# A decoder layer on one core: the second norm's sum formed where the residual's whole rows lie

## The chip, the core and the metric

One NeuronCore of a Trainium2 chip runs the whole program. TensorE (PE) multiplies matrices into PSUM, VectorE (DVE) and ScalarE (ACT) do elementwise work, GpSimd (POOL) does some elementwise work on SBUF and issues transfers, and the SP queue issues transfers only. The metric is the device time of one execution in microseconds (us); the lower, the better.

## The reference

One layer of a hybrid decoder over 2048 new prompt rows and 64 sample rows (8 sequences of 8), width 1024:

```
h = rmsnorm(x, pre_mix_w)
m = mixer(h)                       # retention heads and gated-delta heads, then w_out
x = x + rmsnorm(m, post_mix_w)     # the first residual sum, x1
h = rmsnorm(x, pre_mlp_w)          # the second norm, h2
f = square(relu(h @ w_up)) @ w_down
y = x + rmsnorm(f, post_mlp_w)
```

All of it is in float32 in effect: each operand of a large product is split into a high part and a low part, and three products are summed. The change touches only the two lines in the middle: x1 and h2.

## The kernel before

**Blocks.** The prompt is cut into four blocks of 512 rows (`Block`, b = 0 to 3), each of four tiles of 128 rows; block 1 also has the 64 sample rows as a fifth tile. `main` runs, for each block, the input projection merged with the MLP of the block before it (`merge(blk.proj(), prev.mlp())`), then `out_proj`, then the last group of the MLP's down projection of the block before (`mlp_down(NG - 1)`). After block 3 its own MLP follows.

**Order.** `Weave` is a planner: generators yield either a latency in ns or a key, and resume when the planner's clock, which matmuls advance, has reached it or the key has been signalled. This writes out TensorE's order by hand, and that order is kept. The instructions of the other engines are ordered by the framework's own scheduler, by priority in the order in which they were written; every engine runs its list in order, and a transfer stands in the list of the engine that issues it.

**Tiles.** `page` gives tiles with a tag. Tags that matter: `xin` (five buffers of half rows) takes first loads of weights, the next block's input, stored mixer rows and residuals; `wpc` (eight buffers) holds split weights; `ahi` and `alo` hold the high and low parts of h2, which the MLP reads, and in block 0 also those of the mixer's output; `fhi` and `flo` hold the MLP's features; `XX`, `mt`, `kv`, `ym` and `Ss` hold the tiles 0 to 4 of m. A new tile of a tag waits until all users of the one before it in that buffer are done.

**Weights.** `load_unit` loads a unit of weights the first time through `xin`, splits it (ACT the high part, POOL the low part) into `wpc`, and stores it to DRAM; later uses load the split form straight into `wpc`. The last group of `w_down` is first used behind the output projection of block 1.

**The output projection.** `out_proj` runs over four units u of 256 columns and the tiles in each. `evac` squares a result on ACT into `sq` and writes m, times the weights of the first norm, on DVE. After its last unit a tile's `norm2` is spawned. It loads the residual's row halves into two `xin` buffers (line 1305, POOL's queue), makes the reciprocal root of the mean square (POOL's power, `rsqrt`), forms x1 in place in m (line 1314), squares it on ACT into PSUM tiles of the tag `mx`, stores x1 to `x1d` for the end of the MLP (line 1316, POOL's queue), scales it in place to h2 (line 1323), transposes it on TensorE (line 1333) and writes high parts on ACT and low parts on DVE (line 1337). Its small numbers lie in `r1`, which has two buffers. `lat` gives the planner's latencies: n0 to n3 between these steps and h2 before the transposes.

**After it.** `finish_half` adds the stored x1 to the MLP's result: its loads of `x1d` also go into `xin` (line 1448).

Of the kernel before, what the change touches and what calls it, by code (L numbers as in the profile page):

```python
# [10 lines left out]
AF = mybir.ActivationFunctionType  # L11
ALU = mybir.AluOpType
AX = mybir.AxisListType

P = 128
D_MODEL = 1024
T = 512
NC = T // P
# [7 lines left out]
KT = D_MODEL // P  # L26
UNIT = 256
NU = 264
# [177 lines left out]
def hybrid_kernel(ctx: ExitStack, tc: tile.TileContext, I, O, NB: int, SB: int):  # L206
    nc = tc.nc
    PS = bass.MemoryType.PSUM
    NTM = T + NS
    WB = 8  # L210
    XB = 5
    LAG = 5
    HP = 100
    W = Weave()
# [13 lines left out]
    def nm(s):  # L228
        uid[0] += 1
        return f"{s}_{uid[0]}"  # L230

    def page(shape, tag, dt=F32, bufs=1):
        return wk.tile(shape, dt, tag=tag, name=nm(tag), bufs=bufs)

    def small(shape, tag, dt=F32, bufs=2):
        return sm.tile(shape, dt, tag=tag, name=nm(tag), bufs=bufs)

    def mm():
        return mmp.tile([P, 512], F32, tag="mm", name=nm("mm"))

    def mx():
        return mxp.tile([P, 512], F32, tag="mx", name=nm("mx"))
# [4 lines left out]
    def cut(t, n, w=1024):  # L247
        return [t[:, i * w:(i + 1) * w] for i in range(n)]
# [3 lines left out]
    def act(out, in_, f, **kw):  # L252
        return A.activation(out, in_, f, **kw)  # L253

    def stt(out, in0, scalar, in1, op0, op1):
        return V.scalar_tensor_tensor(out=out, in0=in0, scalar=scalar, in1=in1, op0=op0, op1=op1)  # L256

    def tt(out, a, b, op, eng=None):
        return (eng or V).tensor_tensor(out=out, in0=a, in1=b, op=op)  # L259
# [87 lines left out]
    def save(left):  # L347
        while len(unsaved) > left:
            nc.sync.dma_start(*unsaved.pop(0))

    def load_unit(name, idx, n, ncol):


        src = I[name]
        for i in idx:
            src = src[i]
        per = 2 if ncol <= NU else 1
        w = per * ncol
        first = (name, idx) not in stored
        if first:  # L360
            stored[name, idx] = [wst.tile([P, 2 * w], F32, tag=nm("ws"), name=nm("ws")) for q in range(n // per)]
        his, los = [], []
        for q in range(n // per):
            fit = lambda t: t.rearrange("p (a c) -> p a c", a=per)
            both = page([P, 4 * NU], "wpc", F32R, bufs=WB)
            hi, lo = fit(both[:, :w]), fit(both[:, w:2 * w])
            flat = both[:, :2 * w].bitcast(F32)
            if first:
                r = fit(page([P, 2 * NU], "xin", bufs=XB)[:, :w])
                nc.sync.dma_start(r, src[:, per * q:per * (q + 1), :])  # L370
                save(LAG)
                act(hi, r, AF.Copy)
                tt(lo, r, hi.bitcast(F32), ALU.subtract, eng=G)
                if NB > 1:
                    unsaved.append((stored[name, idx][q], flat))
            else:
                save(0)
                nc.sync.dma_start(flat, stored[name, idx][q])
            his.append(hi)
            los.append(lo)  # L380
        return (lambda k: his[k // per][:, k % per, :]), (lambda k: los[k // per][:, k % per, :])
# [43 lines left out]
    class Block:  # L425
# [828 lines left out]
        def out_proj(self, then=None):  # L1254
            tiles, nt = self.tiles, self.nt
            wB = []
            order = self.order
            for e in order[:6]:
                yield self.key(f"m{e}")
            for n, src in enumerate(("post_mix_w", "pre_mlp_w")):  # L1260
                w = page([P, D_MODEL], "kq", bufs=2) if self.b else page([P, D_MODEL], atag[n])
                nc.gpsimd.dma_start(w, I[src].to_broadcast([P, D_MODEL]))
                wB.append(w)
            m = []
            sq = small([P, 5, 4], "sq", bufs=1)

            def evac(ps, t, rows, u):
                act(mx()[:rows, :UNIT], ps[:rows, :UNIT], AF.Square, accum_out=sq[:rows, t, u:u + 1])
                cols = slice(u * UNIT, (u + 1) * UNIT)
                tt(m[t][:rows, cols], ps[:rows, :UNIT], wB[0][:rows, cols], ALU.mult)  # L1270

            for u in range(4):
                wu = load_unit("w_out", (u,), KT, UNIT)
                if u == 1 and then:
                    W.spawn(then(), W.t)
                held = []
                if u == 0:
                    for t, (c0, rows) in enumerate(tiles[:MMB]):
                        ps = mm()
                        yield from gemm_tm(ps[:rows, :UNIT], self.mix, wu, c0, rows, order[:6], last=False)  # L1280
                        held.append(ps)
                    for e in order[6:]:
                        yield self.key(f"m{e}")
                    m += [page([P, D_MODEL], htag[t]) for t in range(nt)]
                for t, (c0, rows) in enumerate(tiles):
                    if t < len(held):
                        ps = held[t]
                        yield from gemm_tm(ps[:rows, :UNIT], self.mix, wu, c0, rows, order[6:], first=False)
                    elif t == NC:
                        ps = yield from gemm_samp(UNIT, self.mix, wu)  # L1290
                    else:
                        ps = mm()
                        yield from gemm_tm(ps[:rows, :UNIT], self.mix, wu, c0, rows, order)
                    evac(ps, t, rows, u)
                    if u == 3:
                        W.spawn(self.norm2(t, m[t], sq, wB), W.t + self.lat["n0"])

        def norm2(self, t, m, sq, wB):
            c0, rows = self.tiles[t]
            mr = m[:rows]  # L1300
            r = small([P, 4], "r1")[:rows]
            rx = lambda i: r[:, i:i + 1]
            xs2 = [page([P, 2 * NU], "xin", bufs=XB)[:rows, :T] for hf in range(2)]
            for hf in range(2):
                nc.gpsimd.dma_start(xs2[hf], self.x_rows(t)[:, hf * T:(hf + 1) * T])
            with tc.high_priority(offset=HP):
                V.tensor_reduce(out=rx(0), in_=sq[:rows, t, :], axis=AX.X, op=ALU.add)
                tsc(rx(0), rx(0), 1.0 / D_MODEL, EPS, ALU.mult, ALU.add)
                rsqrt(rx(0), rx(0), 1)
            yield self.lat["n1"]  # L1310
            for hf in range(2):
                x = xs2[hf]
                mh = mr[:, hf * T:(hf + 1) * T]
                stt(mh, mh, rx(0), x, ALU.mult, ALU.add)
                act(mx()[:rows, :T], mh, AF.Square, accum_out=rx(2 + hf))
            nc.gpsimd.dma_start(self.x1d[c0:c0 + rows, :], mr)
            yield self.lat["n2"]
            with tc.high_priority(offset=HP):
                tt(rx(1), rx(2), rx(3), ALU.add)
                tsc(rx(1), rx(1), 1.0 / D_MODEL, EPS, ALU.mult, ALU.add)  # L1320
                rsqrt(rx(1), rx(1), 1)
            yield self.lat["n3"]
            stt(mr, mr, rx(1), wB[1][:rows], ALU.mult, ALU.mult)
            if t == self.nt - 1:
                W.signal(self.key("w"))
            yield self.lat["h2"]
            if t == 0:
                self.h2 = (page([P, KT, NTM], "ahi", F32R), page([P, KT, NTM], "alo", F32R))
            hhi, hlo = self.h2
            for kk in range(2):  # L1330
                pt = mx()
                for k in range(4):
                    transpose(pt[:, k * rows:(k + 1) * rows], mr[:, (4 * kk + k) * P:(4 * kk + k + 1) * P], rows)
                pv = pt[:, :4 * rows].rearrange("p (k i) -> p k i", k=4)
                hv = hhi[:, 4 * kk:4 * kk + 4, c0:c0 + rows]
                act(hv, pv, AF.Copy)
                tt(hlo[:, 4 * kk:4 * kk + 4, c0:c0 + rows], pv, hv.bitcast(F32), ALU.subtract)
            W.signal(self.key(f"h{t}"), 1.6 * US)
            if t == self.nt - 1:
                W.signal(self.key("n"))  # L1340
# [74 lines left out]

        def mlp(self):
            for g in range(NG):
                yield (self.key("h0"),) if g == 0 else ()
                yield from self.mlp_up(g)
                if g < NG - 1:  # L1420
                    yield ()
                    yield from self.mlp_down(g)
# [141 lines left out]
```

## Time and profile before

| | |
|---|---|
| Median of 3 runs | 2990.23 us (2987.69 to 2990.53) |
| Profiled execution | 2994.72 us, span 2992.9 us |
| TensorE busy | 2869.1 us, 96% of the span |
| DVE, ACT, POOL busy | 49%, 32%, 28% |
| Mean granted clock of TensorE | 0.98 of full speed |
| DMA traffic | 197 GB/s over the span |

A busy TensorE is not TensorE at its peak, since matmuls overlap. The clock has two levels, 1.2 and 2.4 GHz; a granted clock of 0.50 is the lower. In the rows below, `a<-b` reads "a is written from b", `L1305` is line 1305 of the kernel, and `X <- Y` in a list of waits means that X stood still until Y was done. L253, L256, L259, L264, L271 and L275 are the helpers for ACT's, DVE's and TensorE's instructions.

### The profile page before, as it was taken

What the parts mean: (1) busy time and instruction counts of PE and PEld (TensorE: products, weight loads), DVE (VectorE), ACT (ScalarE), POOL (GpSimd) and SP (SyncE); (2) the same over time, 40 slices, a digit from 0 to 9 for tenths busy, and PEclk for the clock granted to TensorE, in tenths of its full rate; (3) what the DMA queues carried; (4) which work ended last, traced back from release to release, by engine and by line L of the source; (5) the groups of instructions that cost most, each with busy time, mean ns of one, the idle gap of its engine ahead of it and who ended that gap; (6) DMA issues with size and microseconds to landing.
All of it is one profiled execution on the core that took longest, in us unless ns stands there. A gap on an engine that the chain in (4) does not pass through costs nothing.

```text
span 2992.9 us, 43660 instructions
## 1 busy us (share of the span) xinstructions
PE 2869.1 (96%) x16392; PEld 2488.7 (83%) x16392; DVE 1457.3 (49%) x3074; ACT 963.9 (32%) x2573; POOL 825.9 (28%) x968
## 2 busy tenths in 40 slices
PE   7999898999999889899999999999999999999998
PEld 6879787787977769788988989988888888888887
DVE  6754466547474572745354444365353534331113
ACT  4555433324343332422323232232222222321111
POOL 6444323536154360602021121131120212210000
PEclk9999898999999999999999999999999999999999
DMA  8454474656646564854445454675555555665554
GB/s 322 173 194 148 168 262 150 237 199 213 217 154 232 177 237 155 312 204 155 170 154 188 149 180 153 225 259 181 176 191 184 183 182 175 239 236 194 185 193 167
DMA packets 190610, 588.94 MB, mean 197 GB/s; under 512 B 26784, under 2 KB 33312, under 8 KB 190400
## 3 DMA queue, kind: packets, MB, share of 16 engines
q1 hardware_dynamic: 157520, 498.36, 47.9%
q0 software_dynamic: 31728, 85.71, 8.6%
q8 instruction: 129, 2.11, 0.3%
q10 hardware_dynamic: 1152, 2.10, 0.2%
q14 instruction: 81, 0.66, 0.1%
HBM read 443.09 MB, written 137.79 MB: 194 GB/s over the span
## 4 chain that ended last, share of the span: by engine, by line
PE 79%; DVE 9%; DMA 4%; issue 3%; POOL 2%; ACT 2%; SPq 0%; DVEq 0%; POOLq 0%; ACTq 0%
PE mm L271 68%; PE mx L271 9%; PE mx L275 2%; DVE XX L259 1%; DVE ym L259 1%; POOL wpc L259 1%; DMA x1d<-mt 1%; DMA xin<-in_w_down 1%; DVE a L259 0%; DMA xin<-in_x_prompt 0%; DMA xin<-in_xpT 0%; DMA XX<-ym 0%; DVE vz L256 0%; ACT junk L253 0%; DVE vzs L256 0%
## 5 line engine op out<-in xcount | busy, mean ns | idle before, releaser
L271 PE MATMUL mm<-ahi,wpc 128*128 128x512 f32 (+2 forms) x3040 | 876.6, 363 | 0.8 <-ACT ahi L253 0.8
L271 PE MATMUL mm<-wpc,fhi 128*128 128x512 f32 x2048 | 654.5, 400 | 13.1 <-DVE a L259 7.4
L271 PEld LDWEIGHTS mm<-ahi,wpc 128*128 128x128 f32 x3040 | 545.2, 190 | 79.5 <-issue 4.8
L271 PE MATMUL mm<-alo,wpc 128*128 128x512 f32 (+2 forms) x1520 | 539.4, 355 | 2.3 <-DVE alo L259 2.3
L271 PEld LDWEIGHTS mm<-wpc,fhi 128*128 128x128 f32 x2048 | 378.9, 189 | 105.9 <-DVE a L259 9.4
L271 PE MATMUL mm<-bhi,wpc 128*128 128x512 f32 (+2 forms) x1536 | 426.7, 353 | 0.0
L271 PE MATMUL mm<-wpc,flo 128*128 128x512 f32 x1024 | 406.2, 397 | 2.4 <-DVE flo L259 2.4
L259 POOL TENSOR_TENSOR wpc<-xin,wpc 128x512 fp32r<-128x512 f32 (+1 forms) x208 | 276.0, 1344 | 218.3 <-ACT wpc L253 197.5
L271 PEld LDWEIGHTS mm<-alo,wpc 128*128 128x128 f32 x1520 | 289.8, 191 | 35.4 <-DVE alo L259 2.7
L253 ACT ACTIVATE raw<-mm 128x512 f32<-128x512 f32 (+2 forms) x226 | 115.5, 511 | 609.4 <-PE mm L271 598.9
L271 PEld LDWEIGHTS mm<-bhi,wpc 128*128 128x128 f32 x1536 | 274.9, 191 | 33.7 <-issue 2.5
L271 PE MATMUL mm<-wpc,bhi 128*128 128x256 f32 (+1 forms) x1664 | 296.5, 284 | 1.2 <-ACT bhi L253 1.2
L259 DVE TENSOR_TENSOR a<-a,mm 128x512 f32<-128x512 f32 x224 | 152.3, 684 | 243.5 <-PE mm L271 243.0
L271 PE MATMUL mm<-blo,wpc 128*128 128x512 f32 (+2 forms) x768 | 266.2, 347 | 0.0
L259 DVE TENSOR_TENSOR flo<-raw,fhi 128x512 fp32r<-128x512 f32 (+1 forms) x166 | 105.6, 636 | 305.6 <-ACT raw L253 305.2
L271 PEld LDWEIGHTS mm<-wpc,bhi 128*128 128x128 f32 x1664 | 250.4, 188 | 1.9 <-ACT bhi L253 1.4
L271 PEld LDWEIGHTS mm<-wpc,flo 128*128 128x128 f32 x1024 | 193.6, 189 | 48.1 <-DVE flo L259 3.3
L271 PE MATMUL mm<-wpc,blo 128*128 128x256 f32 (+1 forms) x768 | 215.2, 280 | 0.4 <-DVE blo L259 0.4
L253 ACT ACTIVATE wpc<-xin 128x512 fp32r<-128x512 f32 (+1 forms) x208 | 130.0, 630 | 185.8 <-PE mm L271 121.3
L271 PEld LDWEIGHTS mm<-blo,wpc 128*128 128x128 f32 x768 | 146.8, 191 | 14.6
L271 PEld LDWEIGHTS mm<-wpc,blo 128*128 128x128 f32 x768 | 144.6, 188 | 0.9 <-DVE blo L259 0.9
L259 POOL TENSOR_TENSOR a<-a,vz 128x512 f32<-128x512 f32 x28 | 36.5, 1318 | 339.3 <-ACT mx L253 339.0
(504 smaller groups left out, 3987.2 us busy)
## 6 DMA issues: line engine op xcount, KB each, us to landing
wpc<-ws SPq DMA_DIRECT2D x612, 512.0 KB, 4.9
ws<-wpc SPq DMA_DIRECT2D x204, 512.0 KB, 5.8
xin<-in_w_up SPq DMA_DIRECT2D x64, 256.0 KB, 5.4
xin<-in_w_down SPq DMA_DIRECT2D x64, 256.0 KB, 5.0
xin<-in_x_prompt POOLq DMA_DIRECT2D x56, 256.0 KB, 5.1
xin<-in_w_ret SPq DMA_DIRECT2D x28, 256.0 KB, 5.0
wpc<-ws SPq DMA_DIRECT2D x12, 528.0 KB, 5.0
mixd<-raw POOLq DMA_DIRECT2D x24, 256.0 KB, 4.6
```

Source lines behind the costliest of these rows:

```text
L253: return A.activation(out, in_, f, **kw)
L259: return (eng or V).tensor_tensor(out=out, in0=a, in1=b, op=op)
L271: return tc.keep_in_program_order(nc.tensor.matmul(out, lhsT, rhs, start=start, stop=stop))
L275: return tc.keep_in_program_order(nc.tensor.transpose(out, in_, ident[:rows, :rows]))
```

## The change

At the start of unit 1 of the output projection one transfer for each tile loads the residual's whole rows, on POOL's queue: in blocks 1 to 3 into the place of `alo` (the sample rows into that of `ahi`), in block 0 into those of `fhi` and `flo`. `norm2` gets its part as `xr`. It forms x1 there in place of in m, squares it and stores it from there, and the scaling writes h2 from `xr` into m. A count `left` signals a new key `x` when the scaling of the last tile has been written out; the transposes of every tile, and the start of the MLP, wait for that key. In blocks 1 to 3 the tiles for h2's parts reuse the residual's places, in block 0 the tiles for the first features do.

```diff
--- before.py
+++ after.py
@@ -1263,6 +1263,7 @@
                 wB.append(w)
             m = []
             sq = small([P, 5, 4], "sq", bufs=1)
+            self.left = nt
 
             def evac(ps, t, rows, u):
                 act(mx()[:rows, :UNIT], ps[:rows, :UNIT], AF.Square, accum_out=sq[:rows, t, u:u + 1])
@@ -1270,6 +1271,16 @@
                 tt(m[t][:rows, cols], ps[:rows, :UNIT], wB[0][:rows, cols], ALU.mult)
 
             for u in range(4):
+                if u == 1:
+
+                    if self.b:
+                        res = cut(page([P, KT * NTM], "alo"), NC)
+                        if self.samp:
+                            res.append(page([P, KT * NTM], "ahi")[:, :D_MODEL])
+                    else:
+                        res = [x for f in ("fhi", "flo") for x in cut(page([P, 2 * D_MODEL], f), 2)]
+                    for t, (c0, rows) in enumerate(tiles):
+                        nc.gpsimd.dma_start(res[t][:rows], self.x_rows(t))
                 wu = load_unit("w_out", (u,), KT, UNIT)
                 if u == 1 and then:
                     W.spawn(then(), W.t)
@@ -1293,37 +1304,38 @@
                         yield from gemm_tm(ps[:rows, :UNIT], self.mix, wu, c0, rows, order)
                     evac(ps, t, rows, u)
                     if u == 3:
-                        W.spawn(self.norm2(t, m[t], sq, wB), W.t + self.lat["n0"])
-
-        def norm2(self, t, m, sq, wB):
+                        W.spawn(self.norm2(t, m[t], sq, wB, res[t]), W.t + self.lat["n0"])
+
+        def norm2(self, t, m, sq, wB, xr):
             c0, rows = self.tiles[t]
             mr = m[:rows]
             r = small([P, 4], "r1")[:rows]
             rx = lambda i: r[:, i:i + 1]
-            xs2 = [page([P, 2 * NU], "xin", bufs=XB)[:rows, :T] for hf in range(2)]
-            for hf in range(2):
-                nc.gpsimd.dma_start(xs2[hf], self.x_rows(t)[:, hf * T:(hf + 1) * T])
             with tc.high_priority(offset=HP):
                 V.tensor_reduce(out=rx(0), in_=sq[:rows, t, :], axis=AX.X, op=ALU.add)
                 tsc(rx(0), rx(0), 1.0 / D_MODEL, EPS, ALU.mult, ALU.add)
                 rsqrt(rx(0), rx(0), 1)
             yield self.lat["n1"]
             for hf in range(2):
-                x = xs2[hf]
+                x = xr[:rows, hf * T:(hf + 1) * T]
                 mh = mr[:, hf * T:(hf + 1) * T]
-                stt(mh, mh, rx(0), x, ALU.mult, ALU.add)
-                act(mx()[:rows, :T], mh, AF.Square, accum_out=rx(2 + hf))
-            nc.gpsimd.dma_start(self.x1d[c0:c0 + rows, :], mr)
+                stt(x, mh, rx(0), x, ALU.mult, ALU.add)
+                act(mx()[:rows, :T], x, AF.Square, accum_out=rx(2 + hf))
+            nc.gpsimd.dma_start(self.x1d[c0:c0 + rows, :], xr[:rows])
             yield self.lat["n2"]
             with tc.high_priority(offset=HP):
                 tt(rx(1), rx(2), rx(3), ALU.add)
                 tsc(rx(1), rx(1), 1.0 / D_MODEL, EPS, ALU.mult, ALU.add)
                 rsqrt(rx(1), rx(1), 1)
             yield self.lat["n3"]
-            stt(mr, mr, rx(1), wB[1][:rows], ALU.mult, ALU.mult)
+            stt(mr, xr[:rows], rx(1), wB[1][:rows], ALU.mult, ALU.mult)
+            self.left -= 1
+            if not self.left:
+                W.signal(self.key("x"))
             if t == self.nt - 1:
                 W.signal(self.key("w"))
             yield self.lat["h2"]
+            yield self.key("x")
             if t == 0:
                 self.h2 = (page([P, KT, NTM], "ahi", F32R), page([P, KT, NTM], "alo", F32R))
             hhi, hlo = self.h2
@@ -1415,7 +1427,7 @@
 
         def mlp(self):
             for g in range(NG):
-                yield (self.key("h0"),) if g == 0 else ()
+                yield (self.key("h0"), self.key("x")) if g == 0 else ()
                 yield from self.mlp_up(g)
                 if g < NG - 1:
                     yield ()
```

## Rows read from the trace of the kernel before

**Rows 1.** The page, part 1: engine, busy us (share of the span), instructions.

```profile
PE 2869.1 (96%) x16392; PEld 2488.7 (83%) x16392; DVE 1457.3 (49%) x3074; ACT 963.9 (32%) x2573; POOL 825.9 (28%) x968
```

**Rows 2.** TensorE's waits, block 1, 1130 to 1260 us: total us, times, longest.

```profile
PE mm L271 <- DVE a L259: 3.8, 1, 3.8
PE mm L271 <- ACT wpc L253: 3.7, 2, 3.2
PE mm L271 <- DVE alo L259: 2.0, 1, 2.0
PE mm L271 <- POOL wpc L259: 1.8, 2, 1.0
```

**Rows 3.** TensorE's waits, block 0, 300 to 450 us.

```profile
PE mm L271 <- DVE mt L259: 3.3, 1, 3.3
PE mx L275 <- DVE ym L256: 2.2, 1, 2.2
...
PE mx L275 <- DVE alo L259: 0.9, 1, 0.9
```

**Rows 4.** TensorE's waits, block 2, 1860 to 1990 us.

```profile
PE mx L275 <- ACT mx L253: 1.7, 1, 1.7
```

**Rows 5.** TensorE's waits, block 3, 2540 to 2660 us.

```profile
PE mx L275 <- ACT mx L253: 1.8, 1, 1.8
```

**Rows 6.** Waits of the SP queue, block 1, 1150 to 1232 us.

```profile
SPq L370 <- DVE mt L256: 23.6, 1, 23.6
```

**Rows 7.** Timeline of the SP queue, block 1.

```profile
1200.52 7.13 SPq L370 DMA_DIRECT2D xin<-in_w_down  x4
```

**Rows 8.** DVE's waits, block 1, 1190 to 1260 us.

```profile
DVE Ss L256 <- DMA xin<-in_x_sample: 5.0, 1, 5.0
```

**Rows 9.** Timeline of DVE, block 3 (start us, us, what, idle before and releaser).

```profile
2608.84 1.29 DVE L256 SCALAR_TENSOR_TENSOR mt<-mt,r,kq 128x1024 f32<-128x1024 f32 x1 [1.06 <-DMA x1d<-mt]
...
2618.07 1.29 DVE L259 TENSOR_TENSOR alo<-mx,ahi 128x512 fp32r<-128x512 f32 x2 [2.58 <-ACT ahi L253]
...
2623.89 1.28 DVE L256 SCALAR_TENSOR_TENSOR ym<-ym,r,kq 128x1024 f32<-128x1024 f32 x1
```

**Rows 10.** Timeline of POOL, block 3.

```profile
2600.82 1.08 POOL L259 TENSOR_TENSOR r<-r,mhalf 128x1 f32<-128x1 f32 x2 [0.51 <-DVE r L264]
...
2614.66 0.55 POOL L1316 DMA_DIRECT2D x1d<-ym  x1 [0.30 <-DVE ym L256]
...
2615.75 0.57 POOL L259 TENSOR_TENSOR r<-r,mhalf 128x1 f32<-128x1 f32 x1
```

**Rows 11.** Stretches after TensorE's waits: engines' busy us, clock, DMA share.

```profile
384.60:391.40 6.80, 5.39 (x25) 5.39 (x26) 4.07 (x8) 1.63 (x8) 4.94 (x8) 0.54 0.94 320
...
429.50:432.90 3.40, 3.40 (x15) 3.40 (x14) 3.40 (x8) 1.14 (x2) 0.00 (x0) 0.50 0.42 152
...
1207.70:1214.60 6.90, 5.29 (x11) 2.94 (x10) 4.60 (x8) 3.26 (x7) 5.27 (x6) 0.51 0.87 312
...
1224.80:1228.20 3.40, 3.40 (x10) 2.62 (x9) 3.40 (x2) 1.83 (x6) 3.38 (x5) 0.50 1.02 393
...
1948.40:1951.80 3.40, 3.40 (x13) 2.81 (x12) 1.12 (x2) 2.26 (x7) 3.38 (x4) 0.50 0.88 298
```

**Rows 12.** Line 1305, the norm's loads of the residual: ns min/median/max.

```profile
L1305 POOL DMA_DIRECT2D xin<-in_x_prompt x32: 536/560/607, 380.3 to 2598.6; - x32
```

**Rows 13.** Line 1316, the stores of the sum: landing times.

```profile
DMA to landing us min/median/max: 3.9/6.5/9.6
```

**Rows 14.** Stretches of the output projections, and after block 3's; same columns.

```profile
1157.00:1168.40 11.40, 11.40 (x98) 11.40 (x98) 3.38 (x8) 2.88 (x12) 0.00 (x0) 1.00 0.62 221
...
2560.00:2571.00 11.00, 10.63 (x88) 10.42 (x89) 2.82 (x6) 2.47 (x11) 0.32 (x1) 1.00 0.70 225
...
2606.00:2620.00 14.00, 12.17 (x61) 9.70 (x60) 9.53 (x16) 6.35 (x18) 6.46 (x8) 1.00 0.95 378
...
348.00:359.00 11.00, 10.42 (x62) 9.94 (x62) 2.56 (x6) 2.43 (x9) 0.00 (x0) 0.71 0.01 1
```

## The prediction

> **What bounds the kernel now.** I read the page first: TensorE is busy for 96% of the span [rows 1], so a change to the norm can only give back time in which TensorE stands still, and the low clock that follows. Next I took the waits of TensorE in the four stretches in which a block's output projection ends and the norm runs: blocks 0, 1, 2 and 3 at about 380, 1200, 1930 and 2600 us. Block 1 has the most: 3.7 + 1.8 us on weights that ACT and POOL split late, 3.8 us on an accumulator that DVE had not added, 2.0 us on low parts [rows 2]. Block 0 has 2.2 + 0.9 us behind the norm and 3.3 us on DVE's `mt` [rows 3]; blocks 2 and 3 have one wait each, 1.7 and 1.8 us, for a PSUM buffer that ACT's squares of the sum hold [rows 4, 5].
>
> Then I asked who was late. In block 1 the SP queue stood 23.6 us at one load into `xin`, waiting for DVE to finish with the residual of `mt` [rows 6]; the four loads of `w_down` behind it were issued from 1200.52 us on [rows 7], and TensorE waited for exactly these weights. Without that wait the first load could have gone at 1200.52 - 23.6 = 1176.9. The 3.8 us come from DVE standing 5.0 us at the sample rows' residual [rows 8], with the accumulators' additions queued behind it. So 5.0 us of DVE cost TensorE 3.8; 1.2 us were slack.
>
> In block 3, DVE's timeline shows the third mechanism [rows 9]. The scaling of `mt` is in place, so it waits until the store of `mt` has been read out and starts at 2608.84. The first reduction of `ym` comes after it by force: `r1` has two buffers, and tile 3 needs tile 1's. POOL had the factor of `mt` ready at 2600.82 + 1.08 = 2601.9 [rows 10]. The chain of tile 3 is thus 2608.84 - 2601.9 = 6.9 us late for a store.
>
> Last, the clock. After each of the waits of blocks 0, 1 (twice) and 2 stands a stretch at the lower level (0.50 or 0.51, 1.2 GHz) [rows 11].
>
> **The change part by part.** *Removed:* 34 loads of half rows on POOL's queue, about 0.56 us of issue each [rows 12], become 17 of whole rows: 17 x 0.56 = 9.5 us of POOL issue. I cost this at nothing, since POOL does not set the pace; what matters is that none of the loads takes one of the five `xin` buffers any more.
>
> *A, the weights of block 1.* With `xin` free of residuals the loads of `w_down` go up to 23.6 us earlier; a landing and two splits do not take that long, so 3.7 + 1.8 = 5.5 us go. The low stretch behind it has 5.29 us of busy matmuls at 0.51 [rows 11]; at the full clock these take half, 2.6 us less. Sum 8.1.
>
> *B, the sample rows.* They are loaded three units of the projection earlier, so DVE finds them: 3.8 us, and half of the next low stretch of 3.40, 1.7. Sum 5.5.
>
> *C, block 0.* The scaling of `ym` no longer waits for its own store: 2.2 + 0.9, and half of 3.40. Sum 4.8. The 3.3 us on `mt` [rows 3] hang on loads of the next block's input, which come before the norm's; I leave them.
>
> *D and E, blocks 2 and 3.* The squares of `ym` come 6.9 us earlier and the PSUM buffers with them: 1.7 + 1.7 in block 2, 1.8 in block 3, where no low stretch follows. Sum 5.2.
>
> *F, late low parts in block 1:* 2.0 us [rows 2], between 0 and 2.0; with the sample chain earlier but a new wait in its place I take half, 1.0.
>
> A to F: 8.1 + 5.5 + 4.8 + 5.2 + 1.0 = 24.6 us.
>
> *Arithmetic:* the same instructions on tiles of the same shape; the sum is written to `x` in place of `m`, at no cost. In the planner's order the new key `x` is set when the last tile has waited n1 to n3, and tile 0 still has its h2 ahead (13.5 to 16.3 us, against 8 to 10 us in which the other tiles end), so the key does not bind and TensorE's order stays.
>
> *Added, the wait on the stores.* In blocks 1 to 3 the residual lies where the low parts will be, so the first low part must wait for every store of the sum and for every scaling. (In block 0 the first features of the MLP wait, after the next block's first projections; I cost that at nothing, and without this cover it would be priced as here.) In block 3 the first low part is written at 2618.07 [rows 9]; without E's wait, at 2616.3. The scaling of `ym` stands at 2623.89, but its factor was there at 2615.75 + 0.57 = 2616.3 [rows 10], and 6.9 earlier that is 2609.4: in time, if DVE takes it ahead of the low parts. The last store was issued at 2614.66 [rows 10]; 6.9 earlier is 2607.8. A store lands 3.9, 6.5 or 9.6 us after issue (smallest, median, largest) [rows 13]: 2611.7, 2614.3 or 2617.4. DVE thus waits 0, 0 or 1.1 us. Queued behind it on DVE are the accumulators' additions, for which TensorE waits; with 1.2 us of slack it pays nothing. The other end, a store that is not issued earlier, is the fourth rival. I stay near 0, but block 1 has a fifth store: 0.5 a block, 1.5 in all.
>
> *Moved, the loads.* 2.1 MB a block (2.4 in block 1) go out while the output projection streams its weights. POOL is idle there (0.00 to 0.32 us busy) and the DMA share is 0.62 and 0.70, in block 0 it is 0.01; in the old place it is 0.95 [rows 14]. In block 1, 221 GB/s at a share of 0.62 is a full rate of 356. If both queues have half, weights get 178 and lack 43 for 2.4 MB / 178 = 13 us, 0.57 MB or 1.6 us; in block 3, 225 / 0.70 = 321, half 161, lacking 64 for 13 us, 0.84 MB or 2.6 us. That is the upper bound for each of three blocks; the lower is 0, for weights are loaded a unit ahead. Nearer to 0 by the free share: I take 1.0 each, 3.0. The Trainium skill says in "DMA: Bandwidth & Descriptors", section "Issuing engines are not separate DMA queues", that DMAs issued from any engine end on the same 16 DMA engines and interleave. By that rule alone the moved loads would slow the weights by the upper bound, and the sum below would be 11.2 in place of 20.1 us; this is the second rival. The share of 0.95 in the old place agrees that the queues share one capacity.
>
> Sum: 24.6 - 1.5 - 3.0 = 20.1 us. The profiled execution took 2994.7 us, 4.5 above the median of the runs shown (0.15%); it would take 2974.6, and the median of 2990.2 goes to **2970**.
>
> **The rivals.**
> 1. *Block 0 gains too* (2964): if the loads that hold back `mt` also come earlier, 3.3 us and half of 5.39 us at 0.54 [rows 11] come on top, 6.0. For it: they wait for `xin` too. Against it: the norm's loads come after them in the queue.
> 2. *Weights wait for the residual* (2979): 1.6 + 2.6 + 2.6 = 6.8 us, and 1.7 for a low stretch after each, 5.1; in place of my 3.0 that is 24.6 - 1.5 - 11.9 = 11.2 faster. Against it: the free share [rows 14].
> 3. *The waits return elsewhere* (2990, within 6): the stretch after the norm is limited by bytes, 0.95 of the DMA engines in block 3 [rows 14], and TensorE, early, waits for weights instead. For it: that share. Against it: TensorE's waits name buffers and, in block 1, loads that were issued late [rows 2, 4, 5]; and the change takes bytes out of this stretch.
> 4. *Slower: the low parts wait for a late last store* (2997). If POOL issues the last store as late as now, 2614.66, behind a load that waits for `xin`, it lands up to 9.6 later at 2624.3. DVE stands 8.0 us at the first low part from 2616.3, TensorE pays 8.0 - 1.2 = 6.8 and 1.7 of clock: 25.5 in three blocks. D, E and F then fall away and A to C, 18.4, stay: 7.1 slower. It decides from 6.1 us a block, a DVE wait of some 5.6 with the clock. Against it: `r1` and the store part 6.9 us earlier, and `xin` has fewer users.
>
> **How the numbers follow.** Chances: the forecast 0.52, rival 1 0.12, rival 2 0.14, rival 3 0.12, rival 4 0.10. A measurement of this kernel tells about 0.2%, 6 us, from no change. Faster: 0.52 + 0.12 + 0.14 = 0.78; same 0.12; slower 0.10. The range begins where all of A to F and rival 1 come at no new cost, 2990 - 30.6 = 2960, and ends at 2988, which takes in rival 2 and the better half of rival 3; rival 4 and the rest of 3 are left out, some 0.16.
>
> **What would show it.** A: no wait of SP at `w_down` for DVE's `mt`, no TensorE wait for `wpc` near 1200. B: no DVE wait for the sample rows. C to E: the scalings of `mt` and `ym` name no store, and the low stretches [rows 11] are gone. New: a wait of the first low part for a store, under 2 us, or for DVE's scaling. I am wrong if TensorE waits for DVE's low parts or accumulators by more than 6 us a block, or for `wpc` during the output projections of blocks 1 to 3.

## The result and the profile after

The changed kernel takes 2967.24 us (median of 4 runs, 2965.26 to 2970.13) against 2990.05 us for the kernel before in the same comparison: 0.9926 of it, 95% interval 0.9913 to 0.9938, 22.8 us faster. The forecast was 2970. The total is right within 3 us, in part by luck: in the traces block 1 gives 3.3 us less than forecast and the other three blocks together 6.3 us more, and the one new wait has another cause than the forecast said.

The page of the changed kernel, part 1, answers to [rows 1]. TensorE is busy for 9.4 us less, and POOL has 17 instructions less, the transfers that were merged.

```profile
PE 2859.7 (96%) x16392; PEld 2483.3 (84%) x16392; DVE 1450.0 (49%) x3074; ACT 964.4 (33%) x2573; POOL 818.3 (28%) x951
```

TensorE's waits of the changed kernel in block 1, 1120 to 1250 us, to be held against [rows 2]. The waits for `wpc` and all but 0.2 us of that for `a` are gone; the waits for low parts (`alo`) have grown from 2.5 us (2.0, and 0.5 in a row below those of [rows 2]) to 4.5 us.

```profile
PE mx L275 <- DVE alo L259: 2.7, 1, 2.7
PE mm L271 <- DVE alo L259: 1.8, 1, 1.8
PE mx L275 <- ACT mx L253: 0.8, 1, 0.8
PE mm L271 <- DVE a L259: 0.2, 1, 0.2
```

TensorE's waits in block 0, 370 to 450 us, against [rows 3]: the 2.2 us for the scaling of `ym` and the 0.9 for `alo` are gone, that for `mt` stays.

```profile
PE mm L271 <- DVE mt L259: 2.7, 1, 2.7
PE mm L271 <- POOL wpc L259: 1.0, 1, 1.0
PE mm L271 <- DMA wpc<-ws: 0.2, 1, 0.2
```

In block 2, 1840 to 1970 us, TensorE waits for nothing; in block 3 the wait of [rows 5] is gone, too. The SP queue's waits in block 1, 1130 to 1215 us, no longer hold the 23.6 us of [rows 6]; what it waits for are split weights that TensorE still reads and first loads that POOL has not yet split:

```profile
SPq L378 <- PE mm L271: 47.6, 9, 12.7
SPq L370 <- POOL wpc L259: 14.0, 3, 13.4
```

and its timeline shows the loads of `w_down`. In the kernel before all eight loads of its last group go out between 1200.52 and 1218.96. In the changed kernel five of them go out between 1095.72 and 1110.83, the last three from 1178.68 to 1181.38:

```profile
1095.72 0.88 SPq L370 DMA_DIRECT2D xin<-in_w_down  x1
...
1110.83 0.76 SPq L370 DMA_DIRECT2D xin<-in_w_down  x1
...
1178.68 0.33 SPq L370 DMA_DIRECT2D xin<-in_w_down  x1
...
1181.38 0.33 SPq L370 DMA_DIRECT2D xin<-in_w_down  x1
```

So the first of them is 104.8 us earlier, and still 93 us earlier against TensorE's work, since block 1 begins 11.6 us earlier in this trace. The forecast had 23.6 us at most.

Three stretches of the changed kernel, same columns as [rows 11]: the clock is now 1.00 where block 0 (at 429.50) and block 2 had a low stretch behind the norm, and in block 1 one remains, behind the new wait. The stretch behind the wait for `mt` in block 0 stays in part (a clock of 0.80 from 384.60 to 391.40).

```profile
421.00:424.40 3.40, 3.40 (x29) 3.39 (x28) 3.40 (x9) 2.65 (x7) 0.00 (x0) 1.00 0.00 0
...
1220.00:1224.00 4.00, 4.00 (x21) 3.66 (x20) 3.97 (x8) 1.75 (x5) 2.66 (x4) 0.57 0.69 277
...
1918.00:1932.00 14.00, 14.00 (x72) 10.95 (x71) 9.53 (x16) 6.33 (x18) 8.90 (x9) 1.00 0.51 191
```

TensorE runs the same 16392 matmuls in the same order in every kernel of this study. So the start of one numbered matmul, minus that of another, gives the length of the same piece of work in each trace. The table has the four norms (matmuls 1980 to 2500, 6330 to 6930, 10050 to 11190 and 14100 to 15000; in the kernel before they start at 357, 1157, 1780 and 2517 us), the rest, and the sum, in us:

| Kernel | block 0 | block 1 | block 2 | block 3 | the rest | sum |
|---|---|---|---|---|---|---|
| before | 78.0 | 100.4 | 172.1 | 145.7 | 2481.3 | 2977.4 |
| after (the changed kernel) | 71.8 | 90.6 | 168.7 | 142.0 | 2478.8 | 2951.9 |
| after_again | 73.9 | 90.5 | 168.6 | 141.6 | 2476.2 | 2950.9 |
| load_alone | 73.1 | 102.5 | 169.7 | 142.6 | 2477.5 | 2965.5 |
| form_alone | 73.2 | 105.8 | 168.5 | 142.4 | 2475.7 | 2965.5 |
| before_r1_five | 73.7 | 101.3 | 169.6 | 141.8 | 2480.4 | 2966.8 |
| before_weights_dve | 76.8 | 96.4 | 170.7 | 145.3 | 2480.8 | 2969.9 |
| after_r1_five | 76.3 | 87.2 | 169.3 | 142.7 | 2477.6 | 2953.2 |
| after_weights_dve | 73.8 | 87.1 | 168.6 | 142.3 | 2481.5 | 2953.4 |
| after_both | 72.3 | 88.0 | 169.3 | 142.7 | 2473.6 | 2945.8 |
| late_load | 77.5 | 89.9 | 168.6 | 142.0 | 2476.3 | 2954.4 |
| load_twice | 73.0 | 91.5 | 168.9 | 145.1 | 2478.0 | 2956.4 |

The norms of the changed kernel are 6.2 + 9.8 + 3.4 + 3.7 = 23.1 us shorter. The rest, in which the change moves nothing, differs by up to 8 us from trace to trace, so single traces tell the stretches apart, and the medians the totals.

### The profile page after: what moved, and what is told of

Its sections match the earlier page's. It is cut to its first block, busy times and chain, and to the rows that moved or that the text cites. A ratio compares the mean times of both kernels' runs of the same rounds, so it can differ in the third digit from the quotient of the medians.

```text
span 2966.9 us, 43631 instructions
## 1 busy us (share of the span) xinstructions
PE 2859.7 (96%) x16392; PEld 2483.3 (84%) x16392; DVE 1450.0 (49%) x3074; ACT 964.4 (33%) x2573; POOL 818.3 (28%) x951
## 4 chain that ended last, share of the span: by engine, by line
PE 80%; DVE 9%; DMA 4%; issue 3%; POOL 2%; ACT 1%; SPq 0%; DVEq 0%; POOLq 0%; ACTq 0%
PE mm L271 69%; PE mx L271 9%; PE mx L275 3%; DVE XX L259 2%; POOL wpc L259 1%; DVE ym L259 1%; DMA xin<-in_w_out 1%; DMA xin<-in_x_prompt 1%; DMA XX<-ym 1%; DMA wpc<-ws 0%; DMA ws<-wpc 0%; DVE a L259 0%; DVE vz L256 0%; DVE Ss L256 0%; DVE blo L259 0%
```

## The experiments

The theory after the result: the forecast's steps A to E hold, and what is lost again in block 1 is not the wait for a store but DVE's last scaling, held while POOL multiplies. The rivals: one half of the change does all of it; the new wait is for a store; the moved loads cost more than they seem to.

**load_alone: the early loads without the new place of the sum.** The sum is formed in m, stored from m and scaled in place, as before.

```diff
-                stt(x, mh, rx(0), x, ALU.mult, ALU.add)
-                act(mx()[:rows, :T], x, AF.Square, accum_out=rx(2 + hf))
-            nc.gpsimd.dma_start(self.x1d[c0:c0 + rows, :], xr[:rows])
+                stt(mh, mh, rx(0), x, ALU.mult, ALU.add)
+                act(mx()[:rows, :T], mh, AF.Square, accum_out=rx(2 + hf))
+            nc.gpsimd.dma_start(self.x1d[c0:c0 + rows, :], mr)
...
-            stt(mr, xr[:rows], rx(1), wB[1][:rows], ALU.mult, ALU.mult)
+            stt(mr, mr, rx(1), wB[1][:rows], ALU.mult, ALU.mult)
```

> The load half of the change alone: whole rows go early to the place of the low parts (block 0: of the features), but the sum is formed in m, stored from m and scaled in place, as before. Theory (two separate mechanisms: buffers of xin for A and B, the store under the scaling for C to E): A and B stay, 8.1 + 5.5 = 13.6 us, with F and the new costs some 11 to 14 us faster than before, 2976 to 2979; the scaling of mt waits for its store in blocks 2 and 3, and TensorE waits there 1 to 2 us for ACT's mx. Rival (the gain is that of the freed stores): at most 5 us faster, 2985 or more. Rival (the load brings all): 2967, as the whole change.

Measured: 2984.04 us, 0.9967 of the kernel before (0.9956 to 0.9977). This is 5 us above the expected total; the kernel before took 2992.74 us in this comparison, so the gain is 8.7 us where 11 to 14 were expected. In block 1 TensorE first gains 13.5 us, nearly as much as with the whole change (14.3), then all of it goes: the block is 2.1 us longer than before. DVE's timeline of load_alone in block 1:

```profile
1211.15 1.28 DVE L256 SCALAR_TENSOR_TENSOR kv<-kv,r,kq 128x1024 f32<-128x1024 f32 x1 [1.63 <-DMA x1d<-kv]
1212.47 0.15 DVE L1315 TENSOR_REDUCE r<-sq 64x1 f32<-64x4 f32 x1
...
1214.88 1.41 DVE L256 SCALAR_TENSOR_TENSOR Ss<-Ss,r,ahi 64x512 f32<-64x512 f32 x2 [0.75 <-POOL r L259]
```

The scaling of tile 2 (`kv`) waits for its store, the sample rows' reduction (tile 4, which needs tile 2's `r1`) comes right behind it. ACT and TensorE of the same kernel:

```profile
1215.72 0.59 ACT L253 ACTIVATE mx<-Ss 64x512 f32<-64x512 f32 x1 [11.08 <-DVE Ss L256]
```

```profile
1217.72 1.54 PE L275 MATMUL mx<-cst,XX 128*128 128x128 f32 x6 [8.92 <-ACT mx L253]
```

ACT stands 11.08 us at the squares of the sample rows, its squares of the MLP's result are queued behind them, and TensorE waits 8.92 us for a PSUM buffer that these hold. With the scaling in place, the wait for the store thus takes back most of what the early loads bring in block 1. A low stretch follows (a clock of 0.50 from 1218 to 1223 us), and the sample rows' scaling takes 6.57 us, of which more below.

Blocks 2 and 3 are not as expected: TensorE waits for no `mx` there, and load_alone gains 2.4 and 3.1 us in them, and 4.9 in block 0, most of what the whole change brings, with the sum still scaled in place. The early loads let the chain start earlier, and the store holds it up less. In block 3 `mt` is stored at 2588.97 and scaled 6.0 us later, with no wait; in the kernel before it is stored at 2599.25 and scaled 9.6 us later [rows 9]. POOL's and DVE's timelines of load_alone:

```profile
2588.97 0.57 POOL L1324 DMA_DIRECT2D x1d<-mt  x1 [0.55 <-DVE mt L256]
```

```profile
2594.92 1.28 DVE L256 SCALAR_TENSOR_TENSOR mt<-mt,r,kq 128x1024 f32<-128x1024 f32 x1
```

**form_alone: the new place of the sum without the early loads.** Half rows come into `xin` as before, the sum is formed there, stored from there in halves and scaled from there.

```diff
-                stt(mh, mh, rx(0), x, ALU.mult, ALU.add)
-                act(mx()[:rows, :T], mh, AF.Square, accum_out=rx(2 + hf))
-            nc.gpsimd.dma_start(self.x1d[c0:c0 + rows, :], mr)
+                stt(x, mh, rx(0), x, ALU.mult, ALU.add)
+                act(mx()[:rows, :T], x, AF.Square, accum_out=rx(2 + hf))
+                nc.gpsimd.dma_start(self.x1d[c0:c0 + rows, hf * T:(hf + 1) * T], x)
...
-            stt(mr, mr, rx(1), wB[1][:rows], ALU.mult, ALU.mult)
+            for hf in range(2):
+                cols = slice(hf * T, (hf + 1) * T)
+                stt(mr[:, cols], xs2[hf], rx(1), wB[1][:rows, cols], ALU.mult, ALU.mult)
```

> The other half alone: the residual still comes as half rows into xin, but the sum is formed, stored (in halves) and scaled from there. Theory: C to E, 10.0 us, come, but xin is now held until the stores have read it, so in block 1 the loads of w_down go out later than 1200 us and A and B grow by up to a store's landing, 6.5 us, and its clock: between 8 us faster and 2 us slower than before, 2982 to 2992. Rival (the freed stores are the whole gain): 2967 to 2972.

Measured: 2984.68 us, 0.9975 (0.9965 to 0.9985), as expected. Blocks 0, 2 and 3 gain 4.8, 3.6 and 3.3 us, nearly what the whole change brings, and block 1 is 5.4 us longer than before. The SP queue's and then TensorE's waits of form_alone there, 1130 to 1215 and 1170 to 1250 us:

```profile
SPq L370 <- DMA x1d<-xin: 25.7, 1, 25.7
```

```profile
PE mm L271 <- ACT wpc L253: 10.8, 2, 7.6
PE mm L271 <- POOL wpc L259: 5.9, 3, 4.2
```

A residual that stays in `xin` until its store has been read out holds `w_down` back still longer than before, 25.7 for 23.6 us, and TensorE waits 16.7 us for weights instead of 5.5. The two halves of the change alone make block 1 longer by 2.1 and 5.4 us; together they make it 9.8 us shorter. In the other three blocks either half alone brings most of the gain.

**before_r1_five: the kernel before, with five buffers for `r1`.** No tile's reduction has to wait for another tile's scaling; nothing else changes.

```diff
-            r = small([P, 4], "r1")[:rows]
+            r = small([P, 4], "r1", bufs=5)[:rows]
```

> The kernel before with five buffers of r1 in place of two, nothing else. Theory: the reduction of tile 3 no longer comes behind the scaling of tile 1, so D and E come in part, 2 to 5 us faster, 2985 to 2988; A and B stay as they were. Rival (r1 is not the gate, DVE is held by the scaling that waits for the store): within 2 us of before. Rival (r1 is all of the 6.9 us): C to E come whole, 10 us faster, 2980.

Measured: 2984.51 us, 0.9973 (0.9963 to 0.9983). The total lies just under the theory's, but the kernel before took 2992.74 us in this comparison, so the gain is 8.2 us: more than the theory's 2 to 5, and nearer to the 10 us of the rival that `r1` is all of it. Block 2 is 2.5 us shorter and block 3 is 3.9, most of what the change has there (3.4 and 3.7), and block 0 4.3 (6.2, and 4.1 in the second trace of the changed kernel). Block 1 gains nothing. So D and E are the chain that [rows 9] showed, scaling behind the store and `r1` behind the scaling, and it gives way wherever it is cut: at `r1` here, at the store in form_alone, by an earlier start in load_alone.

**after_again, late_load, load_twice: what the loads cost.** after_again is the changed kernel once more. In late_load the loads are written in front of unit 3 instead of unit 1; in load_twice each is issued twice.

```diff
-                if u == 1:
+                if u == 3:
```

```diff
-                        nc.gpsimd.dma_start(res[t][:rows], self.x_rows(t))
+                        for again in range(2):
+                            nc.gpsimd.dma_start(res[t][:rows], self.x_rows(t))
```

> The changed kernel unaltered, as the measure for the others of this group: 2967 us, 0.9926 of before.

> The changed kernel, with the loads of the residual at the start of unit 3 in place of unit 1 of the output projection. Theory (the free buffers of xin and the free store bring the gain; but a load must land before its tile's sum, and now it goes out 3 us before the first result): DVE waits 3 to 6 us at the first sum of each block, the chains of all tiles are later by that, and 4 to 10 us of the gain are lost, 2971 to 2977. Rival (POOL issues the loads early wherever they are written, because nothing but the place holds them): 2967.

> The changed kernel with every residual load issued twice, the second the same as the first. It prices the moved bytes. Theory (the output projections have DMA capacity left): no wait of TensorE for wpc in the projections of blocks 1 to 3, at most 3 us slower than the changed kernel, 2967 to 2970. Rival 2 of the prediction (weights wait for the residual): the price per load of 6.8 us and the clock show a second time, 2974 to 2979, with waits for wpc.

Measured: after_again 2968.05 us (0.9924, 0.9910 to 0.9937), late_load 2967.71 (0.9923, 0.9910 to 0.9935), load_twice 2973.76 (0.9949, 0.9936 to 0.9961). late_load is the same as the changed kernel, as its rival had it, since POOL issues the loads when it did before: first and last start of line 1283 in blocks 1 to 3, first in the changed kernel, then in late_load.

```profile
L1283 POOL DMA_DIRECT2D alo<-in_x_prompt x12: 527/527/572, 1137.3 to 2530.3; - x12
```

```profile
L1283 POOL DMA_DIRECT2D alo<-in_x_prompt x12: 527/528/572, 1139.4 to 2533.2; - x12
```

They go out when TensorE has read the old low parts for the last time, wherever the line is written. So this experiment did not move the loads, and tells nothing on what a late load would cost.

load_twice takes 5.7 us more than after_again, next to its rival's total (2974 to 2979), but not for its reason: in blocks 1 to 3 no matmul waits for `wpc`, and in block 3, 2532 to 2544 us, the DMA engines are full. That stretch, and POOL's timeline in it:

```profile
2532.00:2544.00 12.00, 9.67 (x66) 8.57 (x65) 3.27 (x7) 3.46 (x11) 5.34 (x10) 0.90 1.02 408
```

```profile
2536.31 0.54 POOL L1284 DMA_DIRECT2D alo<-in_x_prompt  x1 [3.23 <-DMA alo<-in_x_prompt]
...
2537.41 1.04 POOL L259 TENSOR_TENSOR so<-so,mhalf 128x4 f32<-128x4 f32 x1
```

POOL stands 3.23 us at a second load that waits for the first, and behind it lies the small root `so` of the gated-delta heads; in after_again it runs at 2533.66. ACT waits 3.24 us for `so` (1.35 in after_again), TensorE for ACT, and block 3 is 145.1 us long against 141.6. So 3.5 of the 5.7 us are the price of the second loads' place in POOL's list, and the bytes made no weights late. How much of the 3.23 us is a first load that lands later because the engines are full, this run does not show.

**after_r1_five, after_weights_dve, after_both: the new wait.** DVE's timeline of the changed kernel in block 1, then POOL's:

```profile
1210.04 8.12 DVE L256 SCALAR_TENSOR_TENSOR Ss<-ahi,r,kq 64x1024 f32<-64x1024 f32 x1 [0.69 <-POOL r L259]
...
1218.88 1.29 DVE L259 TENSOR_TENSOR alo<-mx,ahi 128x512 fp32r<-128x512 f32 x2 [0.20 <-ACT ahi L253]
```

```profile
1208.06 0.58 POOL L1324 DMA_DIRECT2D x1d<-ahi  x1 [1.81 <-DVE ahi L256]
...
1209.98 3.79 POOL L259 TENSOR_TENSOR a<-a,vz 128x512 f32<-128x512 f32 x3
1213.72 0.79 POOL L1105 DMA_DIRECT2D XX<-in_rope  x1
1214.53 2.54 POOL L259 TENSOR_TENSOR a<-a,vz 128x512 f32<-128x512 f32 x2
```

The scaling of the sample rows, 1.27 us long in after_both, takes 8.12 us while POOL weights five halves of block 0's MLP result, and ends 1.1 us after the last of them (1210.04 + 8.12 = 1218.16; 1214.53 + 2.54 = 1217.07). All low parts lie behind it, and DVE names no store there. The two cures: `r1` with five buffers, as above, so that the tiles' chains come in another order; and block 0's weighting on DVE, which leaves POOL only the small roots and the transfers there.

```diff
-            tt(av[:, half[u]], src, self.w3[:rows, half[u]], ALU.mult, eng=V if t == NC or tail and u else G)
+            tt(av[:, half[u]], src, self.w3[:rows, half[u]], ALU.mult, eng=V if t == NC or tail and u or self.b == 0 else G)
```

> The changed kernel with five buffers of r1. With the store gone from under the scaling, r1 holds back only tile 4 of block 1, behind the scaling of tile 2. Theory: the sample rows' sum and scaling come 2 to 4 us earlier in block 1, ahead of POOL's weighting of the MLP's result, and the wait of TensorE for low parts there (2.7 us and a low stretch of 3.4 us) shrinks: 1 to 4 us faster than the changed kernel, 2963 to 2966. Rival (POOL's weighting holds the scaling wherever it comes): 2966 to 2969.

> The changed kernel, with the weighting of block 0's MLP result (eight half rows of four tiles) moved from POOL to DVE. In the changed kernel the scaling of the sample rows takes 8.12 us on DVE in block 1 while POOL runs five weightings of 1.3 us, and the first high and low parts come behind it. Theory (POOL's elementwise work holds DVE's scaling): the scaling takes 1 to 3 us, TensorE's waits of 0.8 and 2.7 us for ACT and the low parts and the low stretch of 3.4 us go; DVE has 8 x 0.7 = 5.6 us more, partly in the way: 1 to 5 us faster than the changed kernel, 2962 to 2966. Rival (the scaling waits for something else, as the store of the sample rows): it stays near 8 us and the time at 2967 or above.

> The changed kernel with five buffers for r1 and with the weighting of block 0's MLP result on VectorE instead of GpSimd. If what is lost in block 1 behind the last scaling is what keeps the kernel from more, both cures together give back some 5 us there: the sample rows' scaling takes under 2.5 us, the first matmul of block 1's MLP starts 4 to 6 us earlier against the changed kernel, and the time is 2961 to 2964. The rival: the distance gained there is taken back later, at the small reductions that the next layer's gates make on VectorE between their transfers (PE waited 0.2 us for the low part flo at 2214 in the changed kernel, 1.9 and 2.1 in the two kernels with one cure each): then the time is 2966 to 2969, the same as the changed kernel's.

Measured: after_r1_five 2966.57 us (0.9906, 0.9891 to 0.9922), after_weights_dve 2969.52 (0.9926, 0.9913 to 0.9938), after_both 2964.89 (0.9917, 0.9903 to 0.9930). DVE's scaling in after_weights_dve:

```profile
1211.37 1.28 DVE L256 SCALAR_TENSOR_TENSOR Ss<-ahi,r,kq 64x1024 f32<-64x1024 f32 x1 [0.46 <-POOL r L259]
```

and TensorE's waits, 1195 to 1250 us:

```profile
PE mm L271 <- DVE alo L259: 2.8, 2, 2.6
PE mx L275 <- ACT mx L253: 0.8, 1, 0.8
PE mm L271 <- DVE a L259: 0.2, 1, 0.2
```

The scaling takes 1.28 for 8.12 us. The wait of 2.7 us before the transposes is gone, and with it the low stretch; the 0.8 for ACT stays, against the expectation, and the wait for low parts behind it is 2.8 for 1.8. From the start of block 1 to the matmul that starts at 1240 us in the kernel before, after_again and after_weights_dve have both gained 13.1 us. At 1246 they stand at 8.8 and 12.8, and at the end of the block at 9.9 and 13.3. So the held scaling is the cause of the new wait: it costs 4.0 us, of which 3.4 are left at the end of the block. With five `r1` block 1 is 3.3 us shorter than in after_again, with both cures 2.5. But five `r1` did not work as expected: the scaling starts later (1216.21), because POOL's root for it stands behind four weightings, and takes 2.31 us.

after_weights_dve's total is 3.5 us above the expected 2962 to 2966 (and after_r1_five's 0.6 above 2963 to 2966). Its rest is 5.3 us longer than that of after_again, but only 2.7 longer than in the first trace of the changed kernel, so part of this is the spread between traces. One place of it, TensorE's waits at 2140 to 2225 us, in the gates of block 3's projection:

```profile
PE mm L271 <- DVE flo L259: 1.9, 1, 1.9
```

There DVE's low part stands behind small reductions, which wait for transfers of their own (`XX<-ym` and `ym<-xf`). Together these waits are 4.6 us in after_again and 5.0 in after_both, where TensorE does not wait; 7.2 in the changed kernel, where it waits 0.2; 8.4 in late_load (1.3), 9.0 here (1.9) and 9.3 in after_r1_five (2.1). So TensorE's wait goes with these transfers and not with how early it comes: after_both comes 4.4 us before after_weights_dve. 2210 to 2220 us is at a clock of 0.83 here. Why the transfers differ stays open. after_both lies 0.9 us above its expected 2961 to 2964, nearer to it than to its rival's; its interval overlaps that of the changed kernel (0.9913 to 0.9938), so none of the three is shown to be faster than the change as it is.

**before_weights_dve: did the same hold cost before?** The same edit of one line, in the kernel before.

> The kernel before with the weighting of block 0's MLP result on VectorE instead of GpSimd, nothing else. The theory: there the sum of block 1's waits is set by the weights' staging and by the scalings' wait for the store, and the long scaling next to GpSimd's weighting (6.60 us at 1225) lies behind them, so this alone is worth 0 to 2 us: 2988 to 2991. The rival: the contention of the two engines was already on the path before, and it alone brings 3 to 5 us: 2985 to 2987.

Measured: 2986.14 us, 0.9988 (0.9979 to 0.9997), so 3.6 us faster, with an interval from 0.9 to 6.3. The total lies with the rival, but the trace does not. In the kernel before the long one was the scaling of tile 3; DVE's timeline, then POOL's first weighting, then TensorE at the end of its wait for `a`:

```profile
1225.21 6.60 DVE L256 SCALAR_TENSOR_TENSOR ym<-ym,r,kq 128x1024 f32<-128x1024 f32 x1
```

```profile
1225.70 2.53 POOL L259 TENSOR_TENSOR a<-a,vz 128x512 f32<-128x512 f32 x2
```

```profile
1224.14 0.73 PE L271 MATMUL mm<-wpc,fhi 128*128 128x512 f32 x2 [3.81 <-DVE a L259]
```

In before_weights_dve the scaling takes 1.27. TensorE's waits for `a` and `alo`, 3.8 and 2.0 us in [rows 2], are 2.9 and 1.5 there. But the wait for `a` ends before the long scaling begins and before POOL weights anything, so the hold has no part in it. Block 1 is 4.0 us shorter, and 2.2 of these are there by the matmul that starts at 1228 us in the kernel before, mostly from the shorter wait for `a` and the low stretch that no longer follows it. Only the other 1.8 come at what lies behind the scaling. So the hold cost the kernel before 1.8 us at most, within the theory's 0 to 2; why the first 2.2 differ stays open.

## Why the prediction came out

**A, weights of block 1: right in outcome, too small in reach.** There is no wait of SP for DVE and none of TensorE for `wpc`. I took the 23.6 us of the SP queue for the most by which the loads could come earlier; the first came 104.8 us earlier. It goes out at 1094.65 in load_alone, too, and at 1193.87 in form_alone, where the residuals stay in `xin`. So it is the residuals in `xin` that kept these loads back, and most of it shows in their place in SP's list, not as a wait. **A and B together:** between the matmuls that start at 1127 and 1232 us in the kernel before, the changed kernel gains 25.9 - 11.6 = 14.3 us; the forecast was 13.6. load_alone gains 13.5 in the same place and form_alone loses 8.1 there, so it is the early loads, which leave `xin` free.

**The new wait: wrong in size and cause.** I forecast 0.5 a block for the low parts' wait on stores. Blocks 2 and 3 have none, and nowhere does DVE wait for a store of the sum. Block 1 gives back 5.8 us of the 14.3 by the matmul at 1246: 1.2 at a wait of 0.8 for ACT that I had not counted, 2.7 for low parts and 1.7 in the stretch at 0.57 behind them. The step that failed is "Added, the wait on the stores": it asks when the stores let the first low part go, and takes DVE's scalings at their usual length. What the first low part waits for is the scaling of the sample rows, which is held for 8.12 us while POOL multiplies. **F, late low parts,** came out in size, 1.3 us behind 1246 for the forecast 1.0; but the wait that I named only went from 2.0 to 1.8, and the 0.5 that [rows 2] does not show went whole. In all block 1 gains 9.8 us, and my terms for it (8.1 + 5.5 + 1.0 - 0.5 - 1.0 = 13.1) were too high by 3.3. Without the hold, in after_weights_dve, it gains 13.3.

The Trainium skill, "SBUF — State Buffer", section "Who interferes with whom", says that a DVE instruction with two SBUF inputs contends with a GpSimd instruction that reads SBUF; its "Summary: rules for kernel authors" says that the second to issue is blocked until the first finishes. The trace agrees on the pair (both operands of the scaling are in SBUF), but the scaling was held through five of POOL's instructions (8.12 us), not one (1.27).

**C, block 0: right in mechanism and size.** Between the matmuls that start at 420 and 433 us in the kernel before, where C's two waits and its low stretch lie, the changed kernel gains 5.1 us in both traces; the forecast was 4.8. load_alone and form_alone gain 5.1 there, too, and before_r1_five 3.1. The block as a whole gains 6.2 us in one trace, 4.1 in the other and 0.5 in late_load, since a wait for split weights (`wpc<-ws`) of 0.2 to 3.1 us comes and goes ahead of C's place. load_twice has none, and before_r1_five, with the loads in their old place, has 1.3, so the moved loads are not what makes it; what does stays open. The 2.7 us for `mt` stay, as I left them, so rival 1 fell.

**D and E, blocks 2 and 3: right in mechanism, E too small.** D is 3.4, as forecast. E is 3.7 for 1.8: 2.0 us go at the wait of [rows 5], and another 1.7 between 2626 and 2640 us, where TensorE waited 0.6 for high parts and 0.3 for low parts that I had not counted. Taking the store from under the scaling is not the only cure: load_alone keeps it there and has 2.4 and 3.1 of these gains.

**The moved loads: cost nothing where I had 3.0.** In blocks 1 to 3 no matmul waits for weights, and with every load issued twice none does either. So rival 2 fell, and with it the upper bound: even at a share of 1.02 in load_twice the weights, which are loaded a unit ahead, did not come late. The loads land after 3.6, 7.6 and 12.2 us (smallest, median, largest), and nothing waits for them.

**The sum.** Forecast 4.8 + 13.1 + 1.9 + 0.3 = 20.1 for blocks 0 to 3, with the costs spread as forecast; measured 6.2 + 9.8 + 3.4 + 3.7 = 23.1. Block 1 gives 3.3 less; the others give 6.3 more, 1.4 in C's block, 1.9 at E and 3.0 by costs that did not come. That the total is so near is the luck of these opposite errors. The other 2.5 us of the trace's 25.5 lie in the rest, where no step of mine acts. Rival 3, waits that return where bytes set the limit, did not come: the wait that did return, in block 1, is for DVE, and that at 2214 us goes with two transfers of the gates and is none in after_both, the earliest there. Rival 4, a wait for a late last store, did not come.

## What to carry to other kernels

When a buffer is held for two reasons (a pool that weights need, an in-place result that a store still reads), price the removal of both together: each half of this change made block 1 longer, and the pair made it 10 us shorter. Where either half alone cuts the chain, as in the other three blocks, the second one adds little. When a wait names an engine, look at how long its instructions take there: one of 6.60 us where its kind takes 1.27 is held by something that the change may leave in place. And for a transfer that an idle engine issues early, look at what stands behind it in that engine's list: in load_twice that cost 3.5 us, while no weights came late. Last, follow a gain from matmul to matmul before believing a cause: more than half of what before_weights_dve gained in block 1 came ahead of the instructions that its edit had moved.

## What was not expected of the hardware

A DVE scaling with both operands in SBUF ran 8.12 us beside five POOL multiplications, 1.28 without them. In three kernels it ended 1.1 us after POOL's last product: here, in load_alone (1219.62 + 6.57 = 1226.19, POOL's end 1225.10), and in the kernel before (1231.81, 1230.72; there one of POOL's four is a split of weights). In after_r1_five, where only one POOL multiplication ran beside it, it took 2.31. POOL's own five took 1.26 to 1.27 us each (3.79 / 3, 2.54 / 2), where the median of all 28 of this kind in the changed kernel is 1.29: only DVE paid.
